# Moving the loads of x, the squares of x and the layer constants to other slots and another queue

## The chip, the cores and the metric

The kernel runs on one core of a Trainium2 chip. The metric is the device time of one execution in microseconds (us); a run takes it several times, and the median counts.

## The reference

A trunk of two layers on x of 256 rows by 2048 columns, float32. Each layer is a root-mean-square norm, one wide input projection, and two branches that are gated and merged:

```python
def hybrid_layer(x, ...):
    proj = rmsnorm(x, norm_g) @ w_in           # 2048 -> 13376 columns, split into nine parts
    y_conv = conv_branch(c_a, c_glu, c_gate, ...) @ w_proj_conv
    y_mla = mla_branch(q_down, kv_down, k_pe, m_gate, cos, sin, ...) @ w_proj_mla
    y = sigmoid(g_conv) * y_conv + sigmoid(g_mla) * y_mla
    return x + y @ w_out
```

The convolution branch is `a * sigmoid(glu)`, a causal depthwise convolution of width 31 over the rows, a layernorm over the channels and a SiLU gate. The attention branch has low-rank queries and keys with a rotary part, whose sine and cosine tables come from `positions`.

## The kernel before

**Tiles and products.** Activations are held transposed, channels on the partitions, as sixteen tiles of 128 channels by 256 rows. Every float32 operand is split into a high and a low part (`hi`, `lo`), and a product is made of three matmuls: high by high, low activation by high weight, high activation by low weight. Weights come in pieces of two channel tiles by 512, 384 or 320 columns (`raw`, up to 512 KB), loaded by SP (`load`, line 253). ACT makes the high part (`split_hi`, 283), DVE the low part by subtraction (`split_lo`, 296). There are five `raw` buffers, four `hi` and three `lo`. Iteration j of the piece loop makes `hi` of piece j+3 and `lo` of piece j+2, issues the load of piece j+7, and then the twelve matmuls of piece j; the low weights are used in the last four of them (with some of them earlier in the last piece of a block).

**Slots.** A piece is a slot. `background` (line 328) runs at the end of an iteration: it counts the slot up, runs what `at_slot(ahead, ...)` (309) has put down for this slot, then hands out steps of the queue `fill`. Each engine's instructions are issued in this written order and stay in it, so that an instruction that waits holds up what was written after it on its engine, and a DMA that waits does so for its queue. `background` also keeps a budget for DVE and ACT: per slot the time of the slot's matmuls less that of the slot's split, less the costs that were given to `at_slot`; a negative budget is carried over, a positive one is not. A `fill` step (convolution, layernorm, gating; DVE) is handed out only while DVE's budget is positive; `assist` gives ACT some of the convolution's taps while its own budget allows. `soon` (316) puts a step into the next slot, and `pay` (321) brings it forward.

**The opening of layer 0.** `products_together` (431) makes four blocks of the input projection: `glu` 0 (512 columns), and three `down` blocks (384, 384, 320). Pieces 0 to 7 take the four blocks together for channel tiles 0 to 3; then come pieces 8 to 13 (`glu` 0, 512 columns, tiles 4 to 15), 14 to 25 (384) and 26 to 31 (320). x comes by DMA into `x_in` (`load_x`, 570): tiles 4, 5 at slot 2, 6, 7 at slot 3, 8 to 11 at slot 5, 12 to 15 at slot 7. `first_h` (644) splits and scales two x tiles, called in `split_hi` of piece 4 and of pieces 8 to 13: ACT makes `h_hi`, DVE `h_lo`, ahead of that piece's `hi`. So tiles 4, 5 belong to piece 8, and 14, 15 to piece 13.

The norm's factor is applied on the results, so the sums of squares may come later: `first_sums` (656) loads x again, untransposed, into eight `xres` tiles of 256 KB (SP, slots 4, 5, 6, 9), and ACT squares them with an accumulator (slots 9, 9, 10, 12). `sum_x` (636) makes `rinv_x` from them on DVE at slot 13, and `glu` 0 is evicted at slot 14 (ACT sigmoid, DVE product into `su`, then a transposition through DRAM by POOL's DMAs into `u_t`, done eight slots later, which puts 32 steps of convolution 0 into `fill`). The first `down` block is evicted at slot 21. The rotary tables are twenty steps, the eighteen on DVE in slots 17 to 34, each charged 0.95. Layer constants are two transfers on SP at slot 10 (`load_consts`, 683): `cst` (273 KB: convolution weights, biases, gains) and `rows` (576 KB, sent to every partition).

**Later in layer 0.** Convolutions 0 to 7 run as `fill` from slot 34 on; behind the last come the layernorm's steps, some of which wait for one another by a number of slots (`mean` three slots after `whole_s1`), then `apply` (times the deviation; ACT's SiLU follows `soon`) and `gated` (times the gate), whose result is split into `ycT` by a step put down with `soon`. The products of `pconv` need `ycT`. They begin with the iteration after slot 276; before their first piece a loop runs `fill` until `gated` has begun, and `before_pconv` (1443) pays the split if it was not yet made. In layer 1 the opening takes two blocks only, x comes transposed from layer 0, and the same `load_consts` is at slot 10.

Of the kernel before, what the change touches and what calls it, by code (L numbers as in the profile page):

```python
# [19 lines left out]
P = 128  # L20
# [41 lines left out]
FIRST_TOGETHER, FIRST_ORDER, FIRST_DOWNS = 2, (3, 1, 0, 2), (3, 1)  # L62
# [69 lines left out]
def trunk(ctx: ExitStack, tc: tile.TileContext, xT, x, g_in, pos, win, wuq, wukv, wpc, wpm, wo, cst, rows, invf, out):  # L132
# [19 lines left out]
    pe, vec, act, gps, sp = (InOrder(e) for e in (nc.tensor, nc.vector, nc.scalar, nc.gpsimd, nc.sync))  # L152
# [100 lines left out]
    def load(i):  # L253
        if i >= len(pieces) or i in loaded:
            return
        ap, n = pieces[i]
        loaded[i] = t = raw_p.tile([P, KS * n], F32, tag="raw", name=f"raw{i}")
        sp.dma_start(t, ap)
# [50 lines left out]
    def at_slot(ahead, f, vec=0.0, act=0.0, first=False):  # L309
        steps.insert(0 if first else len(steps), (clock[0] + ahead, (vec, act), f))  # L310
# [162 lines left out]
    def stat_of(hi, lo):  # L473
        return lambda k, t: (hi[:, k, t * P : (t + 1) * P], lo[:, k, t * P : (t + 1) * P])
# [95 lines left out]
    def load_x(engine, a, b):  # L570
        engine.dma_start(x_in[:, a:b, :], xT[:, a:b, :])
# [8 lines left out]
    load(3)  # L580
    load_x(sp, 2, 4)
    load(4)
    for slot, (a, b) in ((2, (4, 6)), (3, (6, 8)), (5, (8, 12)), (7, (12, 16))):
        at_slot(slot, lambda a=a, b=b: load_x(sp, a, b))


    warm = tp_p.tile([P, 256], F32, tag="tp", name="warm")
# [68 lines left out]
    def first_sums(t, c):  # L656

        xts = []

        def begin():  # L660
            for a in (c, c + 1):
                xts.append(wide_p.tile([P, 512], F32, tag="w", name="xres"))
                sp.dma_start(xts[-1], x[t, :, a * 512 : (a + 1) * 512])

        def end():
            for a, xt in zip((c, c + 1), xts):
                junk = work.tile([P, 512], F32, tag="junk", name="junk")
                act.activation(junk, xt, AF.Square, accum_out=ss_x[:, t, a : a + 1])

        return begin, end  # L670


    for l in range(DEPTH):
        last_layer = l == DEPTH - 1
        C = layer_c.tile([P, C_N], F32, tag="cst", name="cst")
# [4 lines left out]
        down = down_row[:, : T * DOWN].rearrange("p (t n) -> p t n", t=T)  # L680
        row = down_row[:, T * DOWN :]

        def load_consts(row=row, C=C, l=l):
            sp.dma_start(C, cst[l])
            sp.dma_start(row, rows[l].partition_broadcast(P))

        qkc = big.tile([P, 2, 8, SEQ], F32R, tag="big", name=f"qkc{l}")
        ss_d = small.tile([P, 3, T], F32, tag="ss_d", name="ss_d")
# [7 lines left out]
        def down_evac(i, t, ps, down=down):  # L696
            at, n = DOWN_BLOCKS[i]
            act.activation(down[:, t, at : at + n], ps, AF.Copy, scale=rinv_x[:, t : t + 1])
# [366 lines left out]
        def glu_evac(b, t, ps, us=us):  # L1065
            r = rinv_x[:, t : t + 1]
            su = wide_p.tile([P, 2, 256], F32, tag="w", name="su")
            sg, u = su[:, 0], su[:, 1]
            act.activation(sg, ps[:, 256:], AF.Sigmoid, scale=r)
            if t == 0:  # L1070
                us[b] = uv_p.tile([P, 2, PAD + SEQ], F32, tag="uv", name="u_t")
                gps.memset(us[b][:, :, :PAD], 0.0)
            at = PAD + t * P

            def product_out():
                vec.scalar_tensor_tensor(u, ps[:, :256], r, sg, op0=ALU.mult, op1=ALU.mult)
                turn(u, 256, lambda z: conv(b) if t == T - 1 else None, us[b][:, :, at : at + P], (0.4, 0.0))

            early.append(product_out)
# [268 lines left out]
        def gmla_evac(c, t, ps, keep=keep):  # L1348
            if c == 0 and t == 0:
                keep["ym"] = big.tile([P, T, D], F32, tag="big", name="ym")  # L1350
            act.activation(keep["ym"][:, t, c * 512 : (c + 1) * 512], ps, AF.Sigmoid, scale=rinv_x[:, t : t + 1])

        def pmla_evac(c, t, ps, keep=keep):
            y = keep["ym"][:, t, c * 512 : (c + 1) * 512]
            vec.tensor_mul(y, ps, y)
# [94 lines left out]
        def rope_table_steps():  # L1450
            tables = rope_tables()
            for a in range(20):
                at_slot(8 + a + (2 if a < 2 else 7), lambda: next(tables, None), 0.0 if a < 2 else 0.95)
# [3 lines left out]
        for kind, i, pl in planned:  # L1457
            if kind == "glu":
                at = 0 if i in (2, 5) else EVAC_AT
                if i == 0 and l == 0:  # L1460
                    at = 6 - 3 * FIRST_TOGETHER
                    for n, (t, c) in enumerate([(0, 0), (0, 2), (1, 0), (1, 2)]):
                        begin, end = first_sums(t, c)
                        at_slot((4, 5, 6, 9)[n], begin)
                        at_slot((9, 9, 10, 12)[n], end, 0.0, 1.5)
                    at_slot(13, sum_x, 2.2)
                elif i == 0:
                    at_slot(8, sum_x, 2.2)
                if i == 0:
                    at_slot(10, load_consts)  # L1470
                if i == 0:
                    if l == 0:
                        rope_table_steps()
                    downs = FIRST_DOWNS[l]
                    products_together(
                        pl, uses_h, lambda i, t, ps: down_evac(i - 1, t, ps) if i else glu_evac(0, t, ps),
                        (at,) + downs * (EVAC_AT,), ((0.9, 2.2),) + downs * ((0.0, 1.0),),
                        homes=("acc", "acc") if l else ("s", "acc", "acc", "tp"),
                    )
                    if downs == len(DOWN_BLOCKS):  # L1480
                        down_after()
                    continue
                product(pl, uses_h, lambda t, ps, i=i: glu_evac(i, t, ps), at, (0.9, 2.2))
            elif kind == "down":
                product(pl, uses_h, lambda t, ps, i=i: down_evac(i, t, ps), costs=(0.0, 1.0))
                if i == len(DOWN_BLOCKS) - 1:
                    down_after()
            elif kind == "uq":
                if i == 0:
                    attention_tiles()  # L1490
                group, block = divmod(i, 3)
                product(pl, of_down(0), lambda t, ps, i=i: uq_evac(i, t, ps), costs=(0.0, (2.9, 2.7, 1.7)[block]))
                at_slot(EVAC_AT + 1, lambda b=GROUP * group + block: rotate_q(b), 1.3)
                if block == 2:
                    at_slot(EVAC_AT + LAST_ROTATE_AT, lambda b=GROUP * group + 3: rotate_q(b), 1.3)
                    attention(GROUP * group + 2)
            elif kind == "ukv":
                product(pl, of_down(4), lambda t, ps, i=i: ukv_evac(i, t, ps), costs=(0.36 * (i % GROUP == 2), 2.6))
                if i % GROUP != 2:
                    attention(i)  # L1500
                if i == NPAIR - 1:
                    layernorm()
            elif kind == "mgate":
                product(pl, uses_h, lambda t, ps, i=i: mgate_evac(i, t, ps), costs=(0.0, 3.5))
            elif kind == "gmla":
                product(pl, uses_h, lambda t, ps, i=i: gmla_evac(i, t, ps), costs=(0.0, 2.7))
            elif kind == "pmla":
                product(pl, stat_of(*keep["o"]), lambda t, ps, i=i: pmla_evac(i, t, ps), costs=(1.25, 0.0))
            elif kind == "gconv":
                product(pl, uses_h, lambda t, ps, i=i: gconv_evac(i, t, ps), costs=(0.0, 3.9))  # L1510
            elif kind == "cgate":
                product(pl, uses_h, lambda t, ps, i=i: cgate_evac(i, t, ps), costs=(0.0, 2.0))
            elif kind == "pconv":
                while "yc" not in keep:
                    run_fill()
                products_together(pl, stat_of(*keep["yc"]), pconv_evac, (EVAC_AT, EVAC_AT, EVAC_AT, 0), (2.4, 0.0), before_pconv, ("acc", "s", "tp", "acc"))
            elif i == 0:
                wout_begin(0)
                wout_begin(1)
                products_together(pl, stat_of(*keep["y"]), wout_evac, (EVAC_AT, EVAC_AT), (1.25, 1.5))  # L1520
            else:
                at_slot(3, lambda i=i: wout_begin(i))
                product(pl, stat_of(*keep["y"]), lambda t, ps, i=i, f=wout_evac: f(i, t, ps),
                        0 if i == 3 else EVAC_AT, (1.25, 1.5),
                        final=last_half if last_layer and i == 3 else None)
# [116 lines left out]
```

## Time and profile before

| | |
|---|---|
| median of 3 runs | 1788.77 us (1788.07 to 1789.15) |
| the profiled execution | 1787.63 us, span 1785.9 us |
| TensorE busy | 1778.5 us (100% of the span) |
| VectorE (DVE) busy | 1537.2 us (86%) |
| ScalarE (ACT) busy | 1295.0 us (73%) |
| GpSimd (POOL) busy | 556.2 us (31%) |
| granted TensorE clock | 1.00 of full speed in every slice |

An engine that is busy for the whole span can still lose time in short stops, and these are read from its list of waits and from its pace. PE is TensorE's matmuls, PEld its weight loads; SPq, POOLq and ACTq are the engines' queues, where DMAs are issued. Starts are us from the span's start. `x3` behind a row means that three instructions of a kind are merged in it, and `[0.4 <-ACT su]` that the engine was idle 0.4 us before it, until that instruction of ACT had ended.

### The profile page before, as it was taken

The numbers are of one execution on the slowest core, as the hardware profiler recorded it, in microseconds if no ns is written. First come the engines' busy times: TensorE is split into PE (matmuls) and PEld (weight loads), VectorE is DVE, ScalarE is ACT, GpSimd is POOL, SyncE is SP. The second block draws the span as 40 slices with busy tenths as digits, with TensorE's granted clock in tenths as the row PEclk, the third lists the DMA queues.
The fourth block names the chain that finished last, engine by engine and source line by source line (L and its number), as shares of the span: only waits on it lengthen the run. The fifth ranks groups of instructions, "written<-read, shape, count | busy, mean of one in ns | idle before, by whom it ended". The sixth has DMA issues, their size and how long they took to land.

```text
span 1785.9 us, 27083 instructions
## 1 busy us (share of the span) xinstructions
PE 1778.5 (100%) x8575; PEld 1575.0 (88%) x8575; DVE 1537.2 (86%) x2486; ACT 1295.0 (73%) x2398; POOL 556.2 (31%) x1009
## 2 busy tenths in 40 slices
PE   9999999999999999999999999999999999999999
PEld 8988888888888888888899888888888888888887
DVE  6899898898999998867669998989899999887674
ACT  7678888988877775745557788898888777666442
POOL 0155565642311110011421555656333111100210
PEclk9999999999999999999999999999999999999999
DMA  8787887887988997678977887778879889866785
GB/s 317 246 278 257 275 281 261 273 292 235 280 249 248 267 253 233 216 239 291 322 251 230 271 284 264 270 267 275 279 253 280 246 248 257 257 213 220 248 281 179
DMA packets 149519, 463.65 MB, mean 260 GB/s; under 512 B 24832, under 2 KB 31232, under 8 KB 149376
## 3 DMA queue, kind: packets, MB, share of 16 engines
q1 hardware_dynamic: 105856, 360.42, 60.1%
q0 software_dynamic: 42928, 100.98, 20.0%
q8 instruction: 67, 1.10, 0.2%
q14 instruction: 76, 0.62, 0.1%
q10 hardware_dynamic: 592, 0.54, 0.1%
HBM read 399.18 MB, written 44.04 MB: 248 GB/s over the span
## 4 chain that ended last, share of the span: by engine, by line
PE 97%; DMA 2%; DVE 0%; ACT 0%; issue 0%; SPq 0%; DVEq 0%; ACTq 0%
PE acc L143 94%; PE s L143 2%; DMA raw<-in_win 1%; PE o_ps L143 1%; DMA x_in<-in_xT 0%; DMA pos_t<-in_pos 0%; DVE lo L143 0%; ACT hi L143 0%; SPq L143 0%; DVE rsq_t L143 0%; DVE xres L143 0%; DVE su L143 0%; ACT su L143 0%; DVE rinv_x L143 0%; PE var L143 0%
## 5 line engine op out<-in xcount | busy, mean ns | idle before, releaser
L143 ACT CAST hi<-raw 128x1024 fp32r<-128x1024 f32 (+3 forms) x682 | 694.6, 1027 | 376.2 <-PE acc L143 291.2
L143 DVE TENSOR_TENSOR lo<-raw,hi 128x1024 fp32r<-128x1024 f32 (+3 forms) x682 | 812.3, 1194 | 145.7 <-PE acc L143 107.4
L143 PE MATMUL acc<-hi,hT 128*128 128x512 f32 (+2 forms) x1728 | 400.8, 373 | 0.4 <-DVE su L143 0.4
L143 PEld LDWEIGHTS acc<-hi,hT 128*128 128x128 f32 x1728 | 320.3, 189 | 40.5 <-PE acc L143 0.7
L143 PE MATMUL acc<-hi,h_hi 128*128 128x512 f32 (+2 forms) x864 | 251.5, 373 | 1.8 <-ACT hi L143 1.7
L143 PE MATMUL acc<-hi,h_lo 128*128 128x512 f32 (+2 forms) x864 | 250.9, 373 | 0.0
L143 DVE SCALAR_TENSOR_TENSOR v_t<-u_t,cst,v_t 128x256 f32<-128x256 f32 x562 | 239.9, 480 | 2.1
L143 PE MATMUL acc<-lo,h_hi 128*128 128x512 f32 (+2 forms) x864 | 220.3, 373 | 0.2 <-DVE lo L143 0.2
L143 PE MATMUL acc<-lo,hT 128*128 128x512 f32 (+2 forms) x864 | 220.3, 373 | 0.0
L143 PEld LDWEIGHTS acc<-hi,h_hi 128*128 128x128 f32 x864 | 160.5, 190 | 23.2 <-ACT hi L143 3.2
L143 PEld LDWEIGHTS acc<-hi,h_lo 128*128 128x128 f32 x864 | 161.8, 189 | 20.2
L143 PEld LDWEIGHTS acc<-lo,h_hi 128*128 128x128 f32 x864 | 161.1, 189 | 20.8 <-DVE lo L143 0.5
L143 PEld LDWEIGHTS acc<-lo,hT 128*128 128x128 f32 x864 | 161.1, 189 | 20.3
L143 POOL DMA_DIRECT2D turn_d<-gate x176 | 95.8, 553 | 218.3 <-DVE gate L143 152.7
L143 POOL DMA_DIRECT2D taps<-taps x71 | 62.4, 879 | 300.1 <-ACT taps L143 227.5
L143 ACT ACTIVATE taps<-u_t,cst 128x256 f32<-128x256 f32 x292 | 128.5, 498 | 0.4 <-DMA taps<-taps 0.4
L143 PE MATMUL acc<-hi,oT 128*128 128x512 f32 x512 | 122.3, 380 | 0.0
L143 PE MATMUL acc<-hi,ycT 128*128 128x512 f32 x512 | 122.3, 379 | 0.0
L143 PE MATMUL acc<-hi,yT 128*128 128x512 f32 x512 | 122.0, 379 | 0.0
L143 POOL DMA_DIRECT2D turned<-turn_d x88 | 50.0, 576 | 211.5 <-ACT hi L143 61.2
L143 PE MATMUL acc<-hi,qkc 128*128 128x512 f32 x448 | 110.4, 380 | 0.0
L143 PEld LDWEIGHTS acc<-hi,oT 128*128 128x128 f32 x512 | 97.0, 189 | 13.5
(179 smaller groups left out, 2363.1 us busy)
## 6 DMA issues: line engine op xcount, KB each, us to landing
raw<-in_win SPq DMA_DIRECT2D x384, 512.0 KB, 4.5
raw<-in_wpm SPq DMA_DIRECT2D x64, 512.0 KB, 4.7
raw<-in_wpc SPq DMA_DIRECT2D x64, 512.0 KB, 4.2
raw<-in_wo SPq DMA_DIRECT2D x64, 512.0 KB, 5.1
taps<-taps POOLq DMA_DIRECT2D x71, 256.0 KB, 6.2
raw<-in_wukv SPq DMA_DIRECT2D x32, 512.0 KB, 4.2
turned<-turn_d POOLq DMA_DIRECT2D x56, 256.0 KB, 5.3
raw<-in_wuq SPq DMA_DIRECT2D x24, 512.0 KB, 4.2
```

The costliest lines, as they stand in the source:

```text
L143: ins = getattr(self.engine, name)(*a, **k)
```

## The change

Three things are moved, and nothing is computed otherwise.

- x is loaded in pairs of tiles, six transfers of 256 KB, at slots 2, 4, 6, 7, 8 and 9.
- The loads of the tiles for the squares go to slots 11, 12, 13 and 17, the squares to 15, 16, 17 and 20, `sum_x` to slot 20, and the eviction of `glu` 0 from slot 14 to slot 21, where the first `down` block is evicted too.
- The two constant transfers are issued by GpSimd instead of SP, each at a slot of its own: 22 and 26 in layer 0, 4 and 7 in layer 1, instead of both at slot 10.

```diff
-    for slot, (a, b) in ((2, (4, 6)), (3, (6, 8)), (5, (8, 12)), (7, (12, 16))):
-        at_slot(slot, lambda a=a, b=b: load_x(sp, a, b))
+    for slot, a in ((2, 4), (4, 6), (6, 8), (7, 10), (8, 12), (9, 14)):
+        at_slot(slot, lambda a=a: load_x(sp, a, a + 2))
...
-        def load_consts(row=row, C=C, l=l):
-            sp.dma_start(C, cst[l])
-            sp.dma_start(row, rows[l].partition_broadcast(P))
+        load_consts = (
+            lambda C=C, l=l: gps.dma_start(C, cst[l]),
+            lambda row=row, l=l: gps.dma_start(row, rows[l].partition_broadcast(P)),
+        )
...
-                    at = 6 - 3 * FIRST_TOGETHER
+                    at = 7
                     for n, (t, c) in enumerate([(0, 0), (0, 2), (1, 0), (1, 2)]):
                         begin, end = first_sums(t, c)
-                        at_slot((4, 5, 6, 9)[n], begin)
-                        at_slot((9, 9, 10, 12)[n], end, 0.0, 1.5)
-                    at_slot(13, sum_x, 2.2)
+                        at_slot((11, 12, 13, 17)[n], begin)
+                        at_slot((15, 16, 17, 20)[n], end, 0.0, 1.5)
+                    at_slot(20, sum_x, 2.2)
                 elif i == 0:
                     at_slot(8, sum_x, 2.2)
                 if i == 0:
-                    at_slot(10, load_consts)
+                    for slot, load_const in zip(((22, 26), (4, 7))[l], load_consts):
+                        at_slot(slot, load_const)
```

`at` is the number of slots between a block's end and its eviction; it was 0 and is 7 for `glu` 0.

## Rows read from the trace of the kernel before

**Rows 1.** The page's first part: busy time, share and instructions of each engine.

```profile
PE 1778.5 (100%) x8575; PEld 1575.0 (88%) x8575; DVE 1537.2 (86%) x2486; ACT 1295.0 (73%) x2398; POOL 556.2 (31%) x1009
```

**Rows 2.** TensorE's waits, whole span: for whom, us in total, times, longest.

```profile
PE acc L143 <- ACT hi L143: 1.7, 3, 1.1
```

**Rows 3.** Windows: length, busy us of each engine (instructions), clock, DMA share, GB/s.

```profile
17.13:24.26 7.13, 7.13 (x38) 6.49 (x38) 4.06 (x6) 3.69 (x6) 0.00 (x0) 1.00 1.03 402
24.26:39.68 15.42, 13.75 (x62) 11.08 (x60) 9.71 (x17) 14.03 (x31) 0.00 (x0) 1.00 0.95 352
39.68:63.59 23.91, 23.66 (x145) 23.37 (x144) 21.63 (x67) 13.30 (x20) 5.68 (x10) 1.00 0.72 233
63.59:73.37 9.78, 9.78 (x74) 9.78 (x73) 8.81 (x25) 7.54 (x11) 0.00 (x0) 1.00 0.85 285
```

**Rows 4.** Timeline of TensorE: first matmuls of pieces 8 and 9.

```profile
21.67 0.60 PE L143 MATMUL acc<-hi,h_hi 128*128 128x512 f32 x2
...
24.26 0.59 PE L143 MATMUL acc<-hi,h_hi 128*128 128x512 f32 x2
```

**Rows 5.** Timeline of ACT: x tiles 8, 9; the first square; x tiles 12, 13.

```profile
25.43 0.91 ACT L143 ACTIVATE h_hi<-x_in,gx 128x256 fp32r<-128x256 f32 x2 [3.87 <-DMA x_in<-in_xT]
...
28.93 0.63 ACT L143 ACTIVATE junk<-xres 128x512 f32<-128x512 f32 x1
...
31.98 0.91 ACT L143 ACTIVATE h_hi<-x_in,gx 128x256 fp32r<-128x256 f32 x2
```

**Rows 6.** DMA issues from 0 to 45 us: count, KB each, median us to landing.

```profile
raw<-in_win SPq DMA_DIRECT2D x10, 384.0 KB, 4.4
xres<-in_x SPq DMA_DIRECT2D x8, 256.0 KB, 7.5
x_in<-in_xT SPq DMA_DIRECT2D x2, 512.0 KB, 8.3
x_in<-in_xT SPq DMA_DIRECT2D x3, 256.0 KB, 6.4
```

**Rows 7.** Timeline of DVE: `sum_x` begins and ends, `glu` products, `lo` 25 and 26.

```profile
39.08 0.16 DVE L143 TENSOR_REDUCE totx<-ss_x 128x2 f32<-128x8 f32 x1
...
41.45 0.16 DVE L143 SCALAR_TENSOR_TENSOR rinv_x<-rsq_t,rinv_x 128x2 f32<-128x2 f32 x1
...
43.49 0.88 DVE L143 SCALAR_TENSOR_TENSOR su<-acc,rinv_x,su 128x256 f32<-128x256 f32 x2 [0.97 <-ACT su L143]
...
58.74 0.95 DVE L143 TENSOR_TENSOR lo<-raw,hi 128x768 fp32r<-128x768 f32 x1
...
60.47 0.82 DVE L143 TENSOR_TENSOR lo<-raw,hi 128x640 fp32r<-128x640 f32 x1
```

**Rows 8.** Timelines at layer 1's start: SP, SP, ACT and TensorE.

```profile
920.28 0.43 SPq L143 DMA_DIRECT2D cst<-in_cst  x1
...
922.09 36.76 SPq L143 DMA_DIRECT2D raw<-in_win  x21
...
928.28 0.83 ACT L143 CAST hi<-raw 128x768 fp32r<-128x768 f32 x1 [3.56 <-DMA raw<-in_win]
...
931.56 1.54 PE L143 MATMUL acc<-hi,hT 128*128 128x384 f32 x8 [0.40 <-DVE su L143]
```

**Rows 9.** Timelines ahead of `pconv`: DVE three times, ACT twice, TensorE.

```profile
725.14 0.68 DVE L143 TENSOR_TENSOR v_t<-v_t,ln_stats 128x512 f32<-128x512 f32 x1
725.74 1.42 DVE L143 TENSOR_TENSOR v_t<-turned,v_t 128x256 f32<-128x256 f32 x4
727.08 1.22 DVE L143 TENSOR_TENSOR lo<-raw,hi 128x1024 fp32r<-128x1024 f32 x1
...
726.67 1.09 ACT L143 ACTIVATE v_t<-v_t,cst 128x256 f32<-128x256 f32 x2
727.66 1.13 ACT L143 CAST ycT<-v_t 128x512 fp32r<-128x512 f32 x2
...
728.92 1.89 PE L143 MATMUL acc<-hi,ycT 128*128 128x512 f32 x8
```

## The prediction

> **What bounds the kernel now.** The busy table comes first: TensorE 1778.5 us of a span of 1785.9 [rows 1]. The second view is TensorE's waits, because a bound engine can only be helped where it stops: the largest entry, ACT's high halves (`hi`), is 1.7 us in three places [rows 2]. That list shows only the idle part. The whole cost of a stop is seen against the pace. Of [rows 3], 9.78 us for six 320-column pieces without a stop is 1.63 us each; [rows 4] give 24.26 - 21.67 = 2.59 us for a 512-column piece, and 7.13 - 2 x 2.59 = 1.95 us for a 384-column one. So 24.26 to 39.68, five 512-column pieces, should take 12.95 us and took 15.42: 2.47 lost. 39.68 to 63.59, twelve 384-column pieces, should take 23.40 and took 23.91: 0.51 lost. Together **2.98 us**: all that the opening of layer 0 has to give.
>
> Why it is lost is read on ACT [rows 5]. At 25.43 it had been idle 3.9 us for x (tiles 8 to 11, one 512 KB transfer); from 28.93 to 31.98 it did four squares (0.76 us each) while piece 12's `hi` stood behind them: TensorE's longest stop, 1.1 us [rows 2]. The x transfers took 8.3 us (512 KB) and 6.4 us (256 KB) to land, the squares' tiles 7.5 [rows 6], in a stretch where DMA was full (402 GB/s at share 1.03 [rows 3]). The 0.51 belongs to DVE: `sum_x` from 39.08 to 41.6, then a wait for ACT's sigmoid until 43.49 [rows 7].
>
> A second place that the change touches is layer 1's start. SP issues `cst` and `rows` at 920.28, the next weight piece at 922.09, and ACT gets that piece only at 928.28 after 3.56 us idle; `glu` block 0's eviction is behind it on ACT, and TensorE stops 0.40 us at 931.56 for the bank [rows 8].
>
> **Part 1, x in pairs.** Two 512 KB transfers become four of 256 KB, at slots 6 to 9 instead of 5 and 7, and tiles 6 and 7 come one slot later; six transfers instead of four cost SP two more issues, which are no bound. The pair for piece p is issued at the end of iteration p-5, where the first tile of each transfer of before went out at the end of iteration p-6; its tiles are split in iteration p-3. It stands on SP behind the weight load of its iteration (piece p+2), which waits for DVE's `lo` of piece p-3. The last pair (14, 15), for piece 13, is the tightest: the load of piece 15 ahead of it waits for `lo` of piece 10, done about 27.2 us if tile 8 comes at about 24.2 (a little ahead of the 25.43 of [rows 5]). It is then issued at 27.7 and must be there 0.82 + 0.94 us of ACT ahead of piece 13, which starts at 34.6 if nothing stops: 32.8. The lead is 5.1 us. By the nearest rows landing takes 6.4 us for 256 KB where DMA is full and 4.4 for the 384 KB pieces [rows 6]. By then the 2 MB of squares' tiles are no longer ahead of it, so I take 4.5 us and no wait; the bounds are 0 and 1.3 us. For pairs 10 and 12 the leads are about 7 us.
>
> [...]
>
> **Part 2, squares later.** Eight squares (0.76 us each, 6.1 us of ACT) and their 2 MB leave the 512-column pieces and go to slots 15 to 20, among 384-column pieces where ACT needs some 0.75 us of 1.95 for `hi`. Three slots running with 1.52 us of squares overdraw ACT by 0.3 us each, against a lookahead of three pieces: nothing. So the 2.47 us are gained in full if x is in time, and the 0.51 too, since `sum_x` is no longer there.
>
> What replaces it: `sum_x` (13 small DVE instructions, 2.5 us [rows 7]) lands in slot 20 and the `glu` product in slot 21, amid the rotary tables, where DVE already spends 1.73 us of every 1.95 (58.74 to 60.47 is one `lo` and one table step, [rows 7]). Let T be piece 19's start, about 46.9. DVE does `lo` 21 until T+0.9 and waits for ACT: `hi` 22, then the last two squares, until T+2.3. `sum_x` ends at T+4.8, the table step at 5.7, `lo` 22 at 6.5; TensorE wants it after eight of twelve matmuls of piece 22, T + 3 x 1.95 + 1.3 = 7.15: in time. Then a table step (7.4) and the two `su` products, which need ACT: the down eviction (1.0, the planner's cost) and then, as before from 41.6 to 43.49, 1.9 us: first at T+7.7, done at 8.8. `lo` 23 is done at 9.7; wanted at 4 x 1.95 + 1.3 = 9.1: **0.6 us** of waiting. After that DVE gains 0.2 us per slot, nothing in the 320-column pieces (0.73 + 0.87 of 1.63), and the two transposes of `u` move to slot 29: 0 to 0.4 us more. I take **0.8 us**. The last squares' tiles are issued at slot 17, about 42.7 to 43; with 4.5 us of landing they arrive when ACT comes to them (47.3), with 7.5 us three later, and each of these microseconds beyond the first half is one of TensorE's. Bounds 0.3 and 3.0.
>
> Part 1 and 2 together: -2.98 + 0.8 = **-2.2 us** (-2.7 to +1.3).
>
> **Part 3, the planner's debt.** The moved costs count in `background`, which hands out the convolution steps (`fill`) only while DVE's budget is positive. A slot of n columns adds 12 (n/2400 + 0.0028) - 0.04 less 2n/960 + 0.06 (the lines of `background`): 1.427 (512 columns), 1.054 (384) or 0.867 (320). Before, `sum_x` (2.2) and `glu` (0.9) are charged at slots 13 and 14, where the allowance is otherwise thrown away (only a negative budget is carried over), and are paid off before the tables begin at slot 17. Now they fall at 20 and 21, where a table step (0.95) leaves 0.104 a slot, then -0.083 with 320 columns. My count: -2.1 after slot 20, -2.9 after 21, -3.4 after 29 (0.8 for the transposes), -2.7 after 34, +0.1 at 36. Before, one step is given out at 34, one at 35, two at 36; now one at 36 with 0.46 less left: 3 x 0.81 + 0.46 = 2.9 us of convolution behind. The queue is never empty until the layer's convolutions are done, so the lag is carried for 200 slots; only ACT's assistance, which takes taps as long as there are some, eats part of it. Carrying the same arithmetic through (convolution steps 0.81 or 0.73, assistance by ACT's budget), the last one ends in slot 254 instead of 253, `whole_s1` falls in 256 instead of 255, and the layernorm's chain, whose steps wait for each other by slots, is one slot late to its end: the first `gated` pair comes out in slot 276 instead of 275.
>
> That slot is the last before `pconv`. Before: `apply` and the four multiplications at 725.14 to 727.1 on DVE, a SiLU pair and the two `ycT` casts on ACT at 726.67 to 728.7, and TensorE takes `ycT` at 728.92 [rows 9]. The cover is a few tenths of a microsecond. One slot later the multiplications begin behind the next `lo`, 727.7, and end at 729.75; the conversion is then no longer a step of slot 276 but is forced by `before_pconv`, behind `hi` (to 729.6), with the owed SiLU ahead of it (1.0 us): first cast done about 731.25. TensorE stops 728.92 to 731.25, 2.3 us, and its second four matmuls wait some 0.3 more for the low half: **+2.6 us**. Bounds: 0, if the lag is below half a slot when the chain starts, and 3.5.
>
> **Part 4, constants by GpSimd.** In layer 0 slots 22 and 26 stand beside the `u` transfers on POOL's queue; the first reader is the first convolution step, slot 36. In layer 1 slots 4 and 7 come behind the two `turned` fetches of slot 4, and POOL has then nothing more until the `su` transfers. Nothing waits for them. They leave the queue ahead of the 922.09 load: without 0.9 MB in front, it lands in about 4 us as others do (4.4 [rows 6]) instead of 6.1, `su` is evicted some 1.8 us sooner, and the stop of 0.40 with its restart (0.1) is gone: **-0.5 us** (0 to -0.5). The earlier slots meet weight loads with two pieces of lookahead; cover if that fails: at most the same 0.5 comes back.
>
> [...]
>
> **Sum.** -2.2 - 0.5 + 2.6 = **-0.1 us** on 1787.63, the profiled execution. The median of the runs before is 1788.77, 1.1 above that execution; I put the same difference on it: **1788.6 us**.
>
> **The rivals.**
> 1. The sum above, gains and the new stop at `pconv` cancelling: 1788.6, chance 0.46. For it: the list of budgets, and 0.2 us of cover in [rows 9]. Against: ACT's assistance is the least sure part of the count.
> 2. `pconv`'s cover holds: -2.7, 1786.1, chance 0.30. For it: a lag of under 1.2 us at slot 255 would leave `whole_s1` where it is.
> 3. Slower: the last x pair is late because landing still takes what the 512 KB transfers took, 8.3 us [rows 6]. Tile 8 then comes at 25.3, piece 10 is 0.5 late, `lo` 10 and with it the pair's issue 1.1 later (28.8), landing 37.1, and piece 13 starts 3.8 late instead of 34.6 + 0.5. Price 0.5 + 3.8, so -2.98 + 4.3 + 0.8 - 0.5 + 2.6 = +4.2: 1793.0. It decides from a landing of about 5 us on; against it, 2 MB less in the queue. Chance 0.11.
> 4. The last squares' tiles are late by 2 us and more (landing 7.5): -2.98 + 3.0 - 0.5 + 2.6 = +2.1, 1790.9. Chance 0.13.
>
> **How the numbers follow.** About 0.2%, 3.6 us, is what a measurement of this kernel can tell from no change. No gain can pass it by much: 2.98 + 0.5 = 3.5 is all there is, so faster has 0.04 (from the second case, if something in the rest of the layer also gains). Slower needs the third case or the fourth with a larger price: 0.11. Same: 0.85. The range takes cases 1, 2 and 4 with their bounds: from -3.2 to +3.2 of 1788.8, 1785.6 to 1792.0.
>
> **What would show it.** TensorE's three stops for `hi` before 40 us gone and piece 13 starting near 34.6; ACT without a wait for `x_in` after tile 8; a stop of 0.3 to 1 us near 54 to 56 for `lo`; the first convolution step two slots later; a stop of TensorE for `ycT`, about 2.6 us, at some 726; the stop at 931 gone. If the stop at `pconv` is missing, my count of the lag is wrong; if there are stops for x between 24 and 35, the landing is.

## The result and the profile after

The changed kernel takes **1791.51 us** (median of 22 executions, 1788.59 to 1792.78) against 1787.82 for the kernel before (22 executions, 1786.61 to 1789.15): a ratio of 1.0019, interval 1.0013 to 1.0026, some **3.7 us slower**. The prediction was 1788.6, no difference that can be measured. The profiled execution after takes 1791.25 us, its span 1789.5. Three executions in a slower state (6742 us of the kernel before, 2339 us of run 2, 7536 us of run 14) are left out of the ratios.

The engines' busy time, and TensorE's list of waits (for whom, us in total, times, longest) after the change:

```profile
PE 1780.2 (99%) x8575; PEld 1573.0 (88%) x8575; DVE 1535.4 (86%) x2481; ACT 1297.3 (72%) x2404; POOL 553.7 (31%) x1015
...
PE acc L143 <- ACT ycT L143: 2.2, 1, 2.2
PE acc L143 <- DVE lo L143: 1.5, 2, 0.8
...
PE acc L143 <- ACT hi L143: 0.4, 1, 0.4
```

The 1.7 us for `hi` of [rows 2] are 0.4. In their place stand 2.2 us for `ycT` and 1.5 for `lo`. That is 2 us more idle, but the time is 3.7 worse: busy time also rose, by 1.7 us against [rows 1], for the same 8575 matmuls. A lower clock would do that; the windows below show one, 0.57.

The TensorE starts of both traces, set side by side matmul by matmul, say where. The difference (after less before) changes by +0.35 by 9.23 us (the first weight pieces landed later: ACT waited 1.31 us for one at 8.13, where it had waited 0.81 at 7.80; the instructions up to there are the same in both kernels), by -0.49, -1.25, -0.42 and -0.41 from 27 to 43 us (all stops of the opening gone), by +0.93, +0.86 and +0.13 from 55 to 72 us (new stops for `lo`), by more than 4 between 729 and 735 us, and by -0.56 at 931 us. Each step has another 0.10 of its sign in the matmul behind it, the restart, which a list of the steps leaves out. So the sums are read from the level of the difference between them: +0.32 ahead of 27 us, -2.66 from 43 to 55, -0.32 from 76 to 729, +4.08 from 740 to 931 and +3.44 behind it (+3.6 by the two spans). That is **-2.98** for the old stops of the opening, **+2.34** for its new ones, **+4.40** at the conv projection and **-0.64** in layer 1.

**The opening**, timelines of SP (issue of x tiles 14, 15) and of ACT (x tiles 8, 12, 14, which answer to [rows 5]), and the DMA issues from 0 to 45 us (count, KB, median us to landing, as in [rows 6]):

```profile
27.82 0.43 SPq L143 DMA_DIRECT2D x_in<-in_xT  x1
...
24.32 0.91 ACT L143 ACTIVATE h_hi<-x_in,gx 128x256 fp32r<-128x256 f32 x2 [1.34 <-DMA x_in<-in_xT]
...
28.67 0.91 ACT L143 ACTIVATE h_hi<-x_in,gx 128x256 fp32r<-128x256 f32 x2 [0.58 <-DMA x_in<-in_xT]
...
31.20 0.91 ACT L143 ACTIVATE h_hi<-x_in,gx 128x256 fp32r<-128x256 f32 x2 [0.68 <-DMA x_in<-in_xT]
...
raw<-in_win SPq DMA_DIRECT2D x14, 384.0 KB, 5.6
...
xres<-in_x SPq DMA_DIRECT2D x8, 256.0 KB, 6.0
x_in<-in_xT SPq DMA_DIRECT2D x7, 256.0 KB, 5.9
```

No chain of squares stands between the tiles any more, and tile 14 is at 31.20, ahead of the 32.8 at which it was wanted. Its transfer, issued at 27.82, landed after 3.4 us. But the 4.5 us of landing did not hold for the rest: in the median the x transfers take 5.9, the tiles of the squares 6.0 (the last ones 6.4), and the 384 KB pieces 5.6 instead of 4.4.

What that does twenty microseconds later: SP's issue of the last squares' tiles, ACT's two squares, DVE's `sum_x`, and TensorE's two stops:

```profile
43.05 0.90 SPq L143 DMA_DIRECT2D xres<-in_x  x2
...
49.53 0.63 ACT L143 ACTIVATE junk<-xres 128x512 f32<-128x512 f32 x1 [0.78 <-DMA xres<-in_x]
50.29 0.63 ACT L143 ACTIVATE junk<-xres 128x512 f32<-128x512 f32 x1
...
51.04 0.16 DVE L143 TENSOR_REDUCE totx<-ss_x 128x2 f32<-128x8 f32 x1 [2.30 <-ACT junk L143]
...
55.36 0.92 PE L143 MATMUL acc<-lo,h_hi 128*128 128x384 f32 x4 [0.77 <-DVE lo L143]
58.28 0.92 PE L143 MATMUL acc<-lo,h_hi 128*128 128x384 f32 x4 [0.70 <-DVE lo L143]
```

DVE stood 2.30 us in front of `sum_x` until ACT had the last square, and two pieces' low halves behind it came late.

**The conv projection**, the lines that answer to [rows 9] (DVE twice, ACT twice, TensorE), and windows (length, busy us of each engine, then the granted clock, DMA share and GB/s):

```profile
727.41 0.69 DVE L143 TENSOR_TENSOR v_t<-v_t,ln_stats 128x512 f32<-128x512 f32 x1
728.02 1.43 DVE L143 TENSOR_TENSOR v_t<-turned,v_t 128x256 f32<-128x256 f32 x4
...
729.37 1.09 ACT L143 ACTIVATE v_t<-v_t,cst 128x256 f32<-128x256 f32 x2
730.36 1.12 ACT L143 CAST ycT<-v_t 128x512 fp32r<-128x512 f32 x2
...
731.02 3.65 PE L143 MATMUL acc<-hi,ycT 128*128 128x512 f32 x8 [2.25 <-ACT ycT L143]
...
731.02:734.90 3.88, 3.86 (x10) 2.82 (x11) 1.27 (x2) 3.21 (x5) 0.00 (x0) 0.57 0.81 270
734.90:745.00 10.10, 10.10 (x48) 8.87 (x47) 6.42 (x8) 5.19 (x5) 0.00 (x0) 1.00 0.47 156
```

The multiplications begin at 728.02 instead of 725.74, one slot late and behind a `lo`. TensorE stands 2.25 us, and then the same eight matmuls that took 1.89 us [rows 9] take 3.65: the granted clock is 0.57 over 731.02 to 734.90, 0.50 in each of the three microseconds from 732 to 735, and 1.00 again behind it. The stop cost 2.4 us and the matmuls behind it 2.0 more. Run 2 below divides the 2.0: 0.4 come with the same stop at full clock, 1.6 with the lower clock.

**Layer 1's start**: GpSimd issues the constants, and the cast ahead of `su`'s eviction, which waited 3.56 us for its transfer at [rows 8], now waits for TensorE's progress instead:

```profile
907.98 0.55 POOL L143 DMA_DIRECT2D cst<-in_cst  x1
...
930.95 0.84 ACT L143 CAST hi<-raw 128x768 fp32r<-128x768 f32 x1 [2.14 <-PE acc L143]
```

It comes at 930.95 where everything is 4.08 us later, so 1.4 us sooner than before, and the stop of 0.40 is gone.

### The profile page after: what moved, and what is told of

Read it like the earlier page. It is cut to its first block, busy times and chain, and to the rows that moved or that the text cites. A ratio compares the mean times of both kernels' runs of the same rounds, so it can differ in the third digit from the quotient of the medians.

```text
span 1789.5 us, 27098 instructions
## 1 busy us (share of the span) xinstructions
PE 1780.2 (99%) x8575; PEld 1573.0 (88%) x8575; DVE 1535.4 (86%) x2481; ACT 1297.3 (72%) x2404; POOL 553.7 (31%) x1015
## 4 chain that ended last, share of the span: by engine, by line
PE 98%; DMA 1%; ACT 0%; DVE 0%; issue 0%; SPq 0%; DVEq 0%; ACTq 0%
PE acc L143 95%; PE s L143 2%; PE o_ps L143 1%; DMA xres<-in_x 0%; DMA raw<-in_win 0%; ACT hi L143 0%; SPq L143 0%; ACT L143 0%; DVE rsq_t L143 0%; ACT v_t L143 0%; DVE xres L143 0%; ACT junk L143 0%; DVE lo L143 0%; DVE rinv_x L143 0%; ACT down L143 0%
## 5 line engine op out<-in xcount | busy, mean ns | idle before, releaser
L143 ACT ACTIVATE taps<-u_t,cst 128x256 f32<-128x256 f32 x302 | 132.8, 498 | 0.3 <-DVE v_t L143 0.3
L143 PEld LDWEIGHTS acc<-hi,ycT 128*128 128x128 f32 x512 | 97.4, 191 | 17.0 <-ACT ycT L143 2.6
```

The costliest lines, as they stand in the source:

```text
L143: ins = getattr(self.engine, name)(*a, **k)
```

## The experiments

Runs are numbered in the order in which they were made; 11 and 12 stand with 2 and 3. Two questions: is the stop at the conv projection the planner's bookkeeping or the moved work; and what makes the new stops in the opening. In each run the kernel before was timed on the same chip; its medians were 1788.03 (runs 1 to 4), 1787.68 (5 to 8), 1787.97 (9 to 12) and 1788.08 (13 to 15).

### 1. The change without the two moved charges

```
-    at_slot(20, sum_x, 2.2)
+    at_slot(20, sum_x)
-    ... ((0.9, 2.2),) + ...
+    ... ((0.9 if l else 0.0, 2.2),) + ...
```

> The changed kernel, with one difference in the planner's bookkeeping: sum_x at slot 20 and the eviction of glu 0 at slot 21 of layer 0 are charged 0 instead of 2.2 and 0.9 us of VectorE's budget, so that the convolution steps are handed out nearly as before. The work and its places in the opening stay as in the changed kernel. Theory 1 (the debt makes the first gated pair one slot late, TensorE stops ahead of pconv and then runs at half clock): the stop at 728 to 731 us and the half clock behind it vanish, 4.4 us, and the kernel is 1.4 us faster than before (0.9 from the opening, 0.5 from layer 1). Theory 2 (the loss is made by the moved transfers and waits of the opening): it stays 3 to 4 us slower than before.

Measured: 1787.02 us, ratio 0.9994 (0.9985 to 1.0003). The wait for `ycT` is gone, the clock behind it full; the opening gains the same 2.98 and loses 2.33 again (steps of 0.58, 0.86 and 0.58); -0.64 in layer 1. Two numbers in the planner's table cost 4.4 us on the chip, with no work added; what they shift is when the convolution's steps are handed out, and with that some taps from DVE to ACT (556 on DVE in the change, 562 here and before).

### 2. The charges alone, on the kernel before

```
+    at_slot(20, lambda: None, 2.2)
+    at_slot(21, lambda: None, 0.9)
```

> The kernel before, with nothing moved: two steps without work are put down at slots 20 and 21 of layer 0, charged 2.2 and 0.9 us of VectorE's budget. Theory 1: the opening is as before, the first convolution step comes at slot 36 instead of 34, the first gated pair at slot 276 instead of 275, TensorE stops about 2.3 us at pconv and loses 2.1 more at half clock: 4.4 us slower than before where both happen, 2.3 where the clock holds. Theory 2: no difference, within 0.5 us.

> The kernel before with nothing but the two charges entered at slots 20 and 21 (2.2 and 0.9, with no work behind them), for its trace. Theory 1 (the planner's debt makes the chain ahead of the conv projection one slot late, and the stop lowers the clock): the opening as in the kernel before (1.7 us of stops for `hi`), a stop of 2.1 to 2.4 us for `ycT` at about 731 to 734, the next eight matmuls at 0.43 us instead of 0.22, in all 4.0 to 4.5 us. Rival (the stop belongs to the moved work): none of it in this trace.

Measured: 1792.17 us, ratio 1.0020 (1.0011 to 1.0029): the bookkeeping alone costs as much as the whole change. The trace is run 11's, one more execution of the same kernel (1790.19 us). TensorE's timeline there, its weight loads (PEld) behind the stop, and a window:

```profile
730.87 2.29 PE L143 MATMUL acc<-hi,ycT 128*128 128x512 f32 x8 [2.25 <-ACT ycT L143]
...
731.59 1.16 PEld L143 LDWEIGHTS acc<-hi,ycT 128*128 128x128 f32 x6 [0.43 <-DVE ycT L143]
...
730.90:734.50 3.60, 3.57 (x15) 2.83 (x16) 1.69 (x3) 3.57 (x5) 0.00 (x0) 1.00 0.74 272
```

The same stop of 2.25 us to the hundredth, and **no** lower clock behind it, where run 11's theory 1 had one with the stop. The eight matmuls take 2.29 us, 0.40 more than [rows 9]: 0.10 of restart, then 0.29 for a second wait, for the low half of `ycT`, with its restart. The whole place costs 2.81 us in this trace and 4.40 in the change's, so the lower clock is worth 1.6. The spread of the timed executions says how often it comes. Each run lists the mean granted clock of its executions:

| kernel | executions at 1.000 | median us | at 0.998 or 0.999 | median us |
|---|---|---|---|---|
| the change | 10 | 1790.55 | 12 | 1792.38 |
| charges alone | 5 | 1790.92 | 5 | 1792.54 |
| squares alone (4) | 4 | 1791.36 | 6 | 1792.39 |
| squares five slots on (8) | 5 | 1787.59 | 6 | 1789.26 |
| without the charges (1) | 11 | 1787.02 | 0 | |

The first four have a stop of more than 2.2 us in their trace. They come in two sorts, about half and half, 1.0 to 1.8 us apart, about the 1.6 of the two traces. The fifth has no such stop and no such execution. The division is not proof for a single execution: a mean of 0.999 also occurs where there is no such stop, in some executions of the kernel before and in 4 of run 13's 11, whose median is 1787.19 against 1787.11 of the other seven.

### 3. TensorE kept busy before the projection, by 20 and by 8 matmuls of zeros

```
+    for _ in range(idle):     # 20 or 8 in layer 0, none in layer 1
+        pe.matmul(pts[0][0][:, :256], zeros[:, :P], zeros, start=True, stop=True)
+    idle = 0
```

> The changed kernel, with 20 matmuls of zeros (256 columns, some 2.2 us together) written ahead of pconv's first product in layer 0, into a bank that this product then starts anew: TensorE has something to do while it waits. Theory 1a (the half clock comes from the stop): the granted clock stays at 1.00 behind the place, pconv's first eight matmuls take 1.9 us instead of 3.65, the wait for ycT shrinks to under 0.4, and the kernel is 1.5 us slower than before instead of 3.4. Theory 1b (the slow matmuls have another cause, such as the transfers beside them): they stay at 3.65 us and the kernel at +3.4.

> The changed kernel with 8 matmuls of zeros (256 columns, 0.9 us in all) ahead of the conv projection's first product in layer 0, so that TensorE stands about 1.4 us there instead of 2.25. Theory 1 (a stop of 1.8 us, as in the run with the pairs alone, leaves the clock at full speed and one of 2.25 does not): no matmul at half rate, 1789.9 to 1790.2, as with 20 such matmuls. Rival (after any stop there the next matmuls are slow): the eight take 3.6 us again, 1791.3 to 1791.7.

Measured: 20 give 1790.1 us (ratio 1.0012, 1.0003 to 1.0021), 8 give 1791.26 (1.0018, 1.0009 to 1.0027). In both traces the clock behind is 1.00 and the eight matmuls take 2.29 us, as in run 11. With 8, TensorE still stands 1.36 us:

```profile
733.35 2.29 PE L143 MATMUL acc<-hi,ycT 128*128 128x512 f32 x8 [1.36 <-ACT ycT L143]
...
733.35:737.00 3.65, 3.62 (x16) 2.87 (x17) 1.73 (x3) 3.62 (x5) 0.00 (x0) 1.00 0.74 267
```

By the ratios 20 bring back 1.3 us and 8 only 0.2, so by the medians the 8 missed what theory 1 gave them. The trace with 8 shows that it isn't the projection: in that execution the opening's new stops took 4.35 us (steps of 2.43, 0.86 and 0.74) where the change's took 2.34. How often the clock fell in the timed executions is not known (2 of 11 with 20 and 4 of 11 with 8 have a lower mean, 12 of 22 of the change), and the intervals of 20 and of the change overlap. Run 11 kept its clock with nothing filled in, so a full clock in these two traces does not show that the filling did it: the gain is likely, not shown.

### 4 to 6. One part at a time

Squares alone (part 2 of the prediction, charges with it), pairs alone (part 1), constants alone (part 4): each is that part of the change's diff on the kernel before, nothing else.

> The kernel before with one part of the change: the squares' loads, the squares, sum_x and the eviction of glu 0 at their new slots; x in its former four transfers, the constants on SP at slot 10. Theory 1: the stops for hi before 40 us mostly go (2.2 us), the two stops for lo near 55 and 58 come (1.8), pconv's stop and half clock come (4.4), layer 1 keeps its stop: 4 us slower than before, so this part holds the whole loss and the other two gain 0.6 together. Theory 2: the loss is divided among the parts, and this one is under 2 us slower.

> Part 1 alone: x in pairs from six slots, everything else as before. Theory 1 (the stops before 40 us come from four squares standing on ACT ahead of `hi`, and x's landing only shifts them): the chain of four squares stays, so the opening gains 0 to 0.8 us and the time is 1787.2 to 1788.2 against 1788.0; TensorE still lists 1.2 to 1.7 us of waits for ACT's `hi`. Theory 2 (the stops come from the 512 KB x transfers landing late): 1.25 us and more of the 2.57 go, time 1786.6 or less, and `hi` all but leaves the list of TensorE's waits. Either way no stop at the conv projection, since no cost is moved.

> Part 3 alone: the layers' constants issued by GpSimd at other slots. Theory 1 (the constants stand ahead of the weight piece that layer 1's first block waits for): TensorE's 0.40 us stop for `su` at 931 us goes, 0.5 to 0.6 us with its restart, nothing else moves: about 1787.5 against 1788.0. Rival (all queues share the same transfers, so another issuer changes nothing): the stop stays and the time is 1788.0.

**Squares alone**: 1791.68 us (1.0021, 1.0011 to 1.0030). The opening gains 0.49, 1.25, 0.42 and 0.41, every bit of the 2.98 with the restarts, *with x still in 512 KB transfers*; stops for `lo` of 0.80 and 0.86; then the stop and the lower clock (4.2 us in all). Its trace has two more stops for `lo` at 815 and 818 us, 1.3 us together, which the traces of runs 7, 11 and 13 have in part and the change's has not:

```profile
730.61 3.65 PE L143 MATMUL acc<-hi,ycT 128*128 128x512 f32 x8 [2.25 <-ACT ycT L143]
...
730.60:734.10 3.50, 3.49 (x9) 2.55 (x10) 1.28 (x2) 3.03 (x4) 0.00 (x0) 0.53 0.84 279
```

**Pairs alone**: 1791.13 us (1.0017, 1.0008 to 1.0027), and neither theory had a loss. TensorE's waits and ACT's tile 8:

```profile
PE acc L143 <- ACT hi L143: 4.3, 4, 1.8
...
27.21 0.91 ACT L143 ACTIVATE h_hi<-x_in,gx 128x256 fp32r<-128x256 f32 x2 [4.11 <-DMA x_in<-in_xT]
```

Tile 8 comes 1.8 us later than at [rows 5]. Its pair goes out one slot after the 512 KB transfer of before, behind 1 MB of squares' tiles: SP issues two of those at 14.68 and two at 16.83, and the pair at 20.58. TensorE loses 1.50, 0.59 and 0.67 us from 27 to 37 us, 2.9 in the trace, 3.4 in the median. So the pairs bring nothing by themselves; only with the squares out of the way are they harmless. The two longest stops, 1.82 and 1.76 us, left the clock at 1.00.

**Constants alone**: 1787.67 us against 1787.68 (0.9996, 0.9988 to 1.0005). The trace shows the stop at 931 us gone, -0.64; the time can't resolve it. All twelve traces with the constants moved have this gain; of the others run 11's has 0.38 of it too, where the same weight piece landed sooner by itself (ACT idle 3.16 us instead of 3.56).

### 7 to 10. What makes the new stops for `lo`

All four start from run 1 (the change without charges). 7: the last squares' tiles issued at slot 15 instead of 17. 8: that, and the squares up to two slots sooner, `sum_x` and the eviction of `glu` 0 two. 9: the last two squares read the tiles of the two before, so their 512 KB are never loaded. 10: `sum_x` and the evictions one slot later.

```
7   at_slot((11, 12, 13, 15)[n], begin)
8   at_slot((11, 12, 13, 15)[n], begin);  at_slot((15, 15, 16, 18)[n], end, 0.0, 1.5);  at_slot(18, sum_x);  at = 5
9   begin, end, xts = first_sums(t, c, xts if n == 3 else None)    # begin only for n < 3
10  at_slot(21, sum_x);  at = 8;  (at,) + downs * (EVAC_AT + 1 - l,)
```

> The changed kernel without the two moved charges (as in the first run of that kind, 1787.0 with 2.0 us of new stops for `lo` at 55, 58 and 72 us), and besides the last squares' tiles issued at slot 15 instead of 17. Theory 1 (the new stops at 55 and 58 come from those tiles landing late: ACT waited for them and DVE 2.2 us for the squares): the tiles are there when ACT comes to them, `sum_x` begins about 1.3 us earlier, at some 49.2, and 1.2 to 1.4 us of the two stops go: 1785.7. Rival (DVE is simply overloaded by `sum_x` among the rotary tables, however early it begins): the stops shrink by no more than 0.4 us, 1786.6 to 1787.0.

> As the run before it, but the squares at slots 15, 15, 16 and 18, `sum_x` at slot 18 and the evictions two slots sooner (five slots later than before instead of seven). Theory 1 (with tiles in time, nothing of the 512-column pieces is lost and DVE's overdraft among the tables is the same wherever it falls): the same as the run before it within 0.4 us, 1785.7, which is 1.3 to 1.9 us better than the changed kernel without its charges and 2.3 better than the kernel before. Rival (squares two slots sooner overdraw ACT behind the 512-column pieces and stop TensorE for `hi` again): 0.5 to 1.2 us slower than the run before it.

> The changed kernel without the two moved charges, and without the last 512 KB of squares' tiles: the last two squares read the tiles of the two before, so part of the row sum is of the wrong columns. Theory 1 (the new stops for `lo` at 55 and 58 us come from transfers: the last tiles, or, where those are issued sooner, the weight pieces behind them in the same full queue): with nothing to wait for, ACT squares at its slot, `sum_x` begins by about 49, and at least 1.2 of the 1.5 us of `lo` stops of that kernel go: 1785.7 to 1786.0 against its 1787.0. Rival (DVE is overdrawn by `sum_x` among the rotary tables whatever the transfers do): 1.1 us or more of the stops stay, 1786.7 to 1787.2.

> The changed kernel without the two moved charges, with `sum_x` and the evictions that need it one slot further on (slots 21 and 22), the loads and squares where they are. Theory 1 (DVE's loss is the 2.2 us that it stands still for the last squares, with a table step and two `lo` behind that wait): DVE does them first, the stand shrinks to 0 to 0.4 us, the `lo` stops of 1.5 us shrink to 0.3 or less: 1785.5 to 1785.9, the best of all versions and about 0.1% below the kernel before. Rival (work amid the tables is too much for DVE): the stops stay within 0.4 us of 1.5, or a stop for an accumulator bank takes their place: 1786.8 to 1787.5.

Measured: 1787.21, 1788.04, 1786.64 and 1786.79 us (ratios 0.9996, 1.0001, 0.9993 and 0.9995, each with an interval of about 0.0009 to either side).

Run 7 refutes "the tile is issued too late": issued sooner, it pushes the weight pieces back. ACT now waits 1.50 us for a weight piece at 49.17 us, and the `lo` stops are 1.14, 0.86 and 0.48 us. The DMA view of 34 to 50 us goes with that: the kernel before moves 241 GB/s there, the change 333, and 385 from 43 us on.

Run 9 takes the last tiles' bytes away altogether and gains 0.4 us on run 1 in the median, within the intervals; 0.53, 0.86 and 0.22 us of stops stay. So these tiles are the smaller part. Transfers are not out of it, though: ACT still waits for the tiles before them, and its casts after that run late and close together:

```profile
41.53 0.63 ACT L143 ACTIVATE junk<-xres 128x512 f32<-128x512 f32 x1 [1.00 <-DMA xres<-in_x]
...
44.55 0.63 ACT L143 ACTIVATE junk<-xres 128x512 f32<-128x512 f32 x1 [0.66 <-DMA xres<-in_x]
...
46.17 2.74 ACT L143 CAST hi<-raw 128x768 fp32r<-128x768 f32 x3
```

Run 10 cuts DVE's standing to 0.46 us and does away with the stops at 55 and 58 us, as theory 1 said; but two stops for `hi`, 0.31 and 0.82 us, come at 70 and 73 us. The second follows a wait of ACT for a weight piece; that the rotary tables, which end late here, hold that piece up was my reading and is not shown. DVE's `sum_x`, ACT's wait and the later of the two stops:

```profile
51.95 0.16 DVE L143 TENSOR_REDUCE totx<-ss_x 128x2 f32<-128x8 f32 x1 [0.46 <-ACT junk L143]
...
72.03 1.04 ACT L143 CAST hi<-raw 128x1024 fp32r<-128x1024 f32 x1 [1.56 <-DMA raw<-in_win]
...
73.13 0.70 PE L143 MATMUL acc<-hi,h_hi 128*128 128x512 f32 x2 [0.66 <-ACT hi L143]
```

Run 8 overshot: two slots sooner, `sum_x` is there 2.92 us before its squares, which wait 1.67 us for their tiles, and one long stop replaces two:

```profile
52.88 0.92 PE L143 MATMUL acc<-lo,h_hi 128*128 128x384 f32 x4 [2.44 <-DVE lo L143]
...
53.60:57.20 3.60, 3.60 (x14) 3.60 (x13) 3.48 (x10) 2.61 (x5) 2.81 (x5) 0.53 0.64 168
57.30:62.00 4.70, 4.70 (x31) 4.70 (x30) 4.43 (x14) 1.46 (x2) 2.76 (x6) 1.00 0.86 252
```

Here the clock falls to 0.53 in quite another place of the kernel, behind a stop of 2.44 us. So the fall is not bound to the projection; what the two places share is the stop ahead of it.

### 13 to 15. The charges kept, the rotary tables moved out of the way

```
-    at_slot(8 + a + (2 if a < 2 else 7), lambda: next(tables, None), ...)
+    at_slot(8 + a + (0 if a < 2 else 4), ...)     # 13;  2 instead of 4 in 14 and 15
     # 15 besides: sum_x and its evictions one slot later, as in 10
```

> The changed kernel, all charges kept, with the rotary tables' steps three slots sooner (slots 14 to 31 instead of 17 to 34). By the planner's arithmetic three table charges of 0.95 then fall where the allowance was thrown away, the first convolution step comes at slot 34 and the first `gated` pair at 275 again. Theory 1 (the stop at the conv projection is the debt's slot and nothing else): no wait for `ycT`, clock full behind it, the two `lo` stops at 55 and 58 us still there (1.4 us), the one at 72 us gone: 1786.4 to 1787.0, 4.5 to 5 us below the changed kernel. Rival (the moved work itself, wherever it is charged, delays the chain): the stop stays, 1790 or more.

> As the run before it with the tables five slots sooner (12 to 29), so that the last two slots of them in the 512-column pieces have 2.6 us each, and the first `gated` pair comes at 274. Theory 1 (overdraft of DVE between slots 20 and 34 sets the stops at 70 to 73 us, its standing for the last squares those at 55 and 58): the former gone, the latter stay at 1.4 to 1.6 us: 1786.2 to 1786.8. Rival (all of them are overdraft): those at 55 and 58 shrink too, 1785.3 to 1785.8.

> As the run before it, with `sum_x` and the evictions that need it one slot further on (21 and 22). Theory 1: DVE no longer stands for the squares in front of a `lo`, so the stops at 55 and 58 go as in the run that moved `sum_x` alone, and those that had come at 70 and 73 there (1.1 us) do not, with the tables out of the way: TensorE's waits in the opening under 0.4 us, 1785.0 to 1785.6, the best of all, 0.12 to 0.15% below the kernel before. Rival (the stops only move on again): 1786.3 to 1787.

Measured: 1787.11, 1787.66 and 1786.96 us (ratios 0.9996, 0.9996 and 0.9994; interval of the last 0.9985 to 1.0003). Run 13 settles the first question from the other side: every charge and every moved instruction stays, the tables' charges fall into slots whose allowance was thrown away, the first `gated` pair is at slot 275 again, and the wait for `ycT` is gone, 4.4 us of the change's loss with it. The `lo` stops stay (0.90 and 0.86), in run 14 too (1.16 and 0.86). Run 15 shows that theory 1 on those was wrong: with `sum_x` one slot later DVE doesn't stand at all in front of it, and the stops have merely moved on by one piece, with 0.33 us for `hi` left at 73.7:

```profile
57.81 0.92 PE L143 MATMUL acc<-lo,h_hi 128*128 128x384 f32 x4 [0.33 <-DVE lo L143]
60.73 0.92 PE L143 MATMUL acc<-lo,h_hi 128*128 128x384 f32 x4 [0.70 <-DVE lo L143]
```

None of the versions can be told from the kernel before by its time: the best ones, 1, 10 and 15, are 0.05 to 0.06% below it with intervals that take in 1.

## Why the prediction was wrong

**The opening's gain: right.** 2.98 us were said to be all that there is, and 2.98 came. The last pair's way holds too: issued at 27.82 (27.7 said), there at 31.20 where 32.8 was wanted, and tile 8 at 24.32 (24.2 said). The six transfers of x took 3.4 to 7.2 us to land, the last of them the 3.4, where 4.5 was said. Run 4 shows that all of the gain belongs to the squares, and none to the pairs. Run 5 adds what the sum did not need: I weighed the pairs only with the squares gone, and so never saw that they cost 2.9 us without that.

**The opening's new stops: wrong size, 2.3 us for 0.8.** The step that failed is DVE's wait for ACT, "`hi` 22, then the last two squares, until T+2.3", T being the start of piece 19: `sum_x` begins at T + 3.8. The rest of that working holds to a tenth. From `sum_x` to the end of `lo` 22 I had 4.2 us (T + 2.3 to T + 6.5); run 9's trace has 4.26 (50.31 to 54.57). TensorE wants that `lo` at T + 7.15, so the first stop should be the delay of `sum_x` behind T, less 2.9. T is read from each TensorE timeline, as here from the change's, the steps from the comparison with the kernel before:

```profile
47.28 0.49 PE L143 MATMUL acc<-hi,h_hi 128*128 128x384 f32 x2
```

| trace | T | `sum_x` begins | T + | less 2.9 | first stop measured |
|---|---|---|---|---|---|
| run 3, 20 matmuls | 47.46 | 50.57 | 3.1 | 0.2 | 0.27 |
| run 9, last tiles never loaded | 46.95 | 50.31 | 3.4 | 0.5 | 0.53 |
| the change | 47.28 | 51.04 | 3.8 | 0.9 | 0.93 |
| run 12, 8 matmuls | 47.07 | 52.34 | 5.3 | 2.4 | 2.43 |

Runs 3 and 12 and the change have the same instructions up to that place. So the stop is set by when the squares are done, and that varies by 2 us between these executions. In the change's trace `hi` 22 begins only at T + 0.6 (47.91), and ACT then waits 0.78 us for the tile. The stretch moves 385 GB/s, where [rows 3] has 402 at a DMA share of 1.03. I had taken 4.5 us of landing, because 2 MB had left the queue *ahead* of it; but those 2 MB are the squares' own tiles, moved into this very stretch. The second stop, 0.86 us in almost every version, is the wait of `su` for ACT and the `lo` behind it, which I had at 0.6. Rival 4 (last tiles late) named the mechanism and gave it 0.13; the first stop is there in every trace with `sum_x` at slot 20, in sizes from 0.3 to 2.4, and only in part from the last tiles: run 9, without them, still has 0.53.

**The planner's debt and the stop: right.** First convolution step in slot 36, first `gated` pair in 276, its multiplications at 728.02 (727.7 said), TensorE's wait 2.25 (2.3 said), the second wait 0.29 (0.3 said, run 11). Runs 1, 2 and 13 show it from three sides. ACT's assistance, the least sure part of the count, took some taps more (DVE has 556 instead of 562), and the chain was a slot late even so; rival 2 falls.

**What follows the stop: missed.** The term was +2.6, the trace has +4.40. Where the clock holds, the same place costs 2.81 (run 11), so the waits were sized right; the step that failed is that I costed the stop at its waits alone and left out that TensorE may run on at a lower clock behind it (0.57 in the change's trace), 1.6 us. Of 22 executions 12 have a lower mean clock and lie 1.8 us above the other ten. So this part of the error is not in every execution, and the median happens to fall on the side that has it.

**Layer 1: right**, -0.64 against -0.5 (run 6 alone the same).

The sum, by the profiled execution: -2.98 + 2.34 + 4.40 - 0.64 = +3.1, where I had -2.98 + 0.8 + 2.6 - 0.5 = -0.1. The difference of 3.2 is 1.8 from the projection, nearly all of it the clock, and 1.5 from the new stops, less 0.1 in layer 1. That the range's upper end, 1792.0, held the median is luck: I added to a median of three executions, 1788.77, and that of 22 executions is 1787.82; as a difference the 3.7 us lie outside my +3.2. The chances were wrong too: only rivals 3 and 4, 0.24 together, lay above the kernel before by a microsecond or more, and no case had the lower clock. Nor was 0.2% the least that can be told: with 22 executions of each the interval is 0.07% to either side.

## What to carry over

A step's charge in a hand-written planner is a change to the kernel: before moving one, ask in which slots its debt is paid off, and what stands at the end of the lag. Work that is moved takes its transfers with it: cost the landing by the load of the stretch that it goes to, not by what leaves the stretch that it comes from (the 384 KB pieces from 0 to 45 us took 5.6 us here instead of 4.4), and when a step in order waits on another engine, write the loss as a delay less a slack, so that one number carries the range. The stop of 2.25 us of the bound engine cost its idle time and, in about half of the executions, some 1.6 us more behind it, so give such a stop two prices and two chances.

## What the chip showed

The granted clock fell behind stops of 2.25 us (in the change and in run 4) and of 2.44 us (in run 8), to 0.53 to 0.57 in the windows behind them. Beside the same place at full clock (run 11, 2.81 us) that cost 1.6 us in the change and 1.4 in run 4; in run 8 the matmuls behind the stop lost 1.7. It stayed at 1.00 behind stops of 1.36 us (run 12), 1.76 and 1.82 us (run 5), but also behind one of 2.25 us (run 11) and one of 2.26 us (run 12's at 56.65 us). So a stop's length alone does not decide it, and the same instructions fall on either side from one execution to the next: 10 executions of the change have a mean clock of 1.000 and 12 a lower one. By the table under run 2 the two sorts lie 1.0 to 1.8 us apart; what decides between them was not shown.
